# A macaron encoder step on one core: the down stages by seven products take their operands back by token halves

## The chip, the core and the metric

The kernel runs on one core of a Trainium2 chip. TensorE (PE) multiplies, VectorE (DVE), ScalarE (ACT) and GpSimd (POOL) work beside it, SyncE (SP) issues most transfers, GpSimd's queue the rest. The metric is the device time of one execution in microseconds (us); lower is better.

## The reference

One layer of a streaming encoder, for 16 meta tokens, 1024 prompt frames and 32 sample frames of 1024 channels:

```python
def half_ffn(x, g, w_gate, w_up, w_down):
    h = rmsnorm(x, g)
    return x + 0.5 * ((jax.nn.silu(h @ w_gate) * (h @ w_up)) @ w_down)

x = half_ffn(x, ffn1_norm, ffn1_w_gate, ffn1_w_up, ffn1_w_down)
h = rmsnorm(x, mix_norm)          # then h @ w_in: attention, HGRN2 branch, gates
x = x + merged @ w_out
x = half_ffn(x, ffn2_norm, ffn2_w_gate, ffn2_w_up, ffn2_w_down)
y = rmsnorm(x, final_norm)        # prompt and sample frames
```

The change touches the two products with `w_down` (2816 x 1024), and the norm that follows each.

## The kernel before

Every fp32 operand is split into a high and a low part, and a product is three matmuls (high x high, high x low, low x high). The two FFNs work by Strassen-like recursion: seven products for a 2 x 2 block product, with sums of operands named A11, S1 to S4 on the weight side and B11, T1 to T4 on the token side (`NAMES`). The tokens of an FFN form four quarters of 268 (first FFN) or 264 columns (second); `b` is the half (two quarters), `th` the quarter in it.

Each FFN is an object of class `Seven` (line 313). `rest` (L479) makes the gate and up products, block pair by block pair (11 of them, `i` = 0 to 10). `send` (L334) turns the result of a block into its seven operands: seven pieces of work in `self.later`, each a split into a staging tile `st` (tags R and st, one buffer each, in turn) and a store to `mid_dram` by GpSimd's queue (L349). They are done between later products, and those of block 10 in `down`.

`down` (L532) multiplies by `w_down`. `home(i)` (L488) loads the seven operands of block i into one of three places (`xh`/`xl` j with j = i mod 3, and one to three tiles more), names 0 to 2 in one transfer and 3 to 5 in another (0 and 1, 2 and 3 for j = 2). `lanes` (L501) loads a tile of `w_down` and makes the splits and sums for two blocks. A `Job` (L539) makes the seven products p1 to p7 for one pair of output blocks (`mp` 0 to 3), for one or two blocks of the inner dimension at a time; with `b` None for both halves, in pairs of PSUM banks (`pu`, `pv`, `pf`), else for one half in single banks (`ps_z`, `ps_o`). After p1 ScalarE copies `pv` to `pu` (L575); `out` (L559) adds results to `acc` by VectorE (L566), or writes them by ScalarE the first time (L569). `run` (L602) interleaves: p6 and p7 of a job stand among p1 to p5 of the next; at the end they are made alone.

Order before: block 0 alone for mp 2 and 3 (b None, pair banks), then steps s = 1 to 9 with blocks s-1 and s, mp 0 and 1 in odd and 2 and 3 in even steps, each step loading block s+1; a residual is added in most steps (L621). Then single banks: for each half four jobs (blocks 9 and 10 for mp 2 and 3, block 10 alone for mp 0 and 1), and after each half `after(b)`. In the first FFN that is `after1` (L810): store x1 and `normalise` (L230) the finished token tiles of 400, 384 and 288 columns; after both halves `between` starts the first scaling, and `project_all` (L829) follows with the first three column blocks of `w_in`. In the second it is `after2` (L1699): for each block of 128 tokens eight transposes, two squares with sums by ScalarE, a scale, two writes of `yt` by VectorE and a store of the output.

`PE` keeps the order of TensorE's matmuls as written (class `InOrder`, L91) where it is on; all other engines' orders are set by a planner from program order, dependencies and free buffers.

## Time and profile before

| | us |
|---|---|
| median of 3 runs | 2516.28 (2516.27 to 2518.82) |
| the profiled execution | 2516.3 |
| its span, first to last instruction | 2514.5 |
| TensorE busy in the span | 2411.5 (96%) |
| VectorE busy | 1680.1 (67%) |
| ScalarE busy | 1019.9 (41%) |
| GpSimd busy | 230.9 (9%) |
| mean granted TensorE clock, share of full speed | 0.985 |

The first down stage runs from 512.6 to 767.2 us of the span, the second from 2229.6 to 2491.4 us, with the output norm of the second half behind it. A busy TensorE is read with care, since matmuls are pipelined; the timelines show the idle time ahead of each instruction in brackets, with what ended it. "Before" a row in time says little on its cause: an engine works its queue in order.

### The profile page before, as it was taken

To read this page: it belongs to the slowest core of one execution; us is meant where nothing else is said; L and a number is where in the kernel's file an instruction comes from. 1 tells how busy PE (TensorE), PEld (TensorE's weight loads), DVE (VectorE), ACT (ScalarE), POOL (GpSimd) and SP (SyncE) were. 2 spreads that over 40 slices of the span, in tenths; PEclk is the share of its full clock that TensorE was granted. 3 is DMA by queue.
4 is the path that set the end of the run, shared out by engine and by line. 5 is a ranking of instruction groups with operands and counts; after the bars stand their busy time and mean duration, and the time that the engine had idled before them with its cause. 6 is when DMAs were issued, how large, how long until landed. Compare 5 with 4: busy or idle time off the path is not lost.

```text
span 2514.5 us, 47920 instructions
## 1 busy us (share of the span) xinstructions
PE 2411.5 (96%) x19500; PEld 2303.7 (92%) x19500; DVE 1680.1 (67%) x3160; ACT 1019.9 (41%) x2113; POOL 230.9 (9%) x461
## 2 busy tenths in 40 slices
PE   6999999989997999999999999999899999989996
PEld 5999999989997998898888888998899999989995
DVE  5876767668775377764666665557876776757775
ACT  6444444442234233332555544333444444443222
POOL 1000100000003012121000000111000000000000
PEclk9999999999998999999999999999999999999997
DMA  7234444487742111111111222522243434387741
GB/s 204 96 139 150 140 151 142 159 342 262 251 145 65 58 44 47 56 50 51 52 44 44 59 61 80 180 94 89 91 146 128 155 139 154 139 302 279 255 166 70
DMA packets 266020, 331.94 MB, mean 132 GB/s; under 512 B 41078, under 2 KB 228726, under 8 KB 260166
## 3 DMA queue, kind: packets, MB, share of 16 engines
q1 hardware_dynamic: 243590, 244.96, 29.9%
q0 software_dynamic: 22208, 83.91, 8.4%
q8 instruction: 153, 2.51, 0.4%
q14 instruction: 69, 0.57, 0.1%
HBM read 213.93 MB, written 114.89 MB: 131 GB/s over the span
## 4 chain that ended last, share of the span: by engine, by line
PE 54%; issue 31%; DVE 7%; POOL 3%; DMA 3%; ACT 2%; SPq 0%; POOLq 0%; DVEq 0%; ACTq 0%
PE ps_mm L103 20%; PE ps_z L103 12%; PE pu L103 6%; PE ps_o L103 5%; PE pf L103 4%; PE pv L103 4%; POOL mid_dram L349 3%; PE ps_tr L103 2%; PE ps_tr L106 2%; DMA mid_dram<-st 1%; DMA raw<-in_ffn_w_down_dram 1%; PE ps_z L106 1%; PE ps_mm L106 1%; DVE wlo L203 1%; DVE xl L235 0%
## 5 line engine op out<-in xcount | busy, mean ns | idle before, releaser
L103 PE MATMUL ps_mm<-xh,whi 128*128 128x384 f32 (+2 forms) x952 | 316.8, 333 | 0.5 <-DVE raw L1392 0.5
L103 PE MATMUL ps_mm<-xh,wlo 128*128 128x384 f32 (+2 forms) x952 | 310.3, 326 | 0.0
L103 PE MATMUL ps_mm<-xl,whi 128*128 128x384 f32 (+2 forms) x952 | 309.9, 326 | 0.0
L219 ACT ACTIVATE whi<-S 128x1024 fp32r<-128x1024 f32 x124 | 131.4, 1060 | 311.3 <-PE pu L103 157.8
L103 PEld LDWEIGHTS ps_mm<-xh,whi 128*128 128x128 f32 x952 | 179.3, 188 | 9.0 <-issue 5.0
L103 PEld LDWEIGHTS ps_mm<-xl,whi 128*128 128x128 f32 x952 | 179.3, 188 | 1.1
L103 PEld LDWEIGHTS ps_mm<-xh,wlo 128*128 128x128 f32 x952 | 179.5, 189 | 0.4
L220 DVE TENSOR_TENSOR wlo<-S,whi 128x1024 fp32r<-128x1024 f32 x124 | 151.7, 1223 | 37.5 <-ACT whi L219 34.8
L220 DVE TENSOR_TENSOR st<-g,st 128x536 fp32r<-128x536 f32 (+1 forms) x154 | 107.6, 709 | 101.2 <-ACT st L219 100.8
L349 POOL DMA_DIRECT2D mid_dram<-st x154 | 82.3, 534 | 904.4 <-DVE st L220 843.5
L1184 DVE TENSOR_TENSOR_SCAN left<-left,oneb 128x512 f32<-128x512 f32 (+6 forms) x112 | 107.4, 959 | 55.0 <-ACT left L119 54.6
L202 ACT ACTIVATE whi<-raw 128x1024 fp32r<-128x1024 f32 x67 | 70.5, 1057 | 175.9 <-PE ps_mm L103 136.3
L219 ACT ACTIVATE st<-g 128x536 fp32r<-128x536 f32 (+1 forms) x154 | 96.9, 642 | 88.4 <-DMA mid_dram<-st 75.1
L220 DVE TENSOR_TENSOR wlo<-raw,whi 128x1024 fp32r<-128x1024 f32 x80 | 76.6, 958 | 73.2 <-ACT whi L219 71.5
L103 PE MATMUL ps_z<-xl1s,whi 128*128 128x268 f32 (+1 forms) x424 | 116.8, 288 | 0.7 <-DVE acc1s L566 0.7
L103 PE MATMUL ps_z<-acc1s,whi 128*128 128x268 f32 (+1 forms) x480 | 106.3, 285 | 0.0
L103 PE MATMUL ps_z<-xh1s,whi 128*128 128x268 f32 (+1 forms) x360 | 102.8, 286 | 0.0
L103 PE MATMUL ps_z<-xh1s,wlo 128*128 128x268 f32 (+1 forms) x360 | 102.6, 285 | 0.0
L103 PE MATMUL ps_z<-xh2s,whi 128*128 128x268 f32 (+1 forms) x352 | 100.3, 285 | 0.9 <-ACT s L454 0.9
L103 PE MATMUL ps_z<-xl2s,whi 128*128 128x268 f32 (+1 forms) x352 | 100.3, 285 | 0.0
L103 PE MATMUL ps_z<-xh2s,wlo 128*128 128x268 f32 (+1 forms) x352 | 100.1, 285 | 0.0
L203 DVE TENSOR_TENSOR wlo<-raw,whi 128x1024 fp32r<-128x1024 f32 x67 | 83.2, 1246 | 25.3 <-ACT whi L202 25.1
(674 smaller groups left out, 7636.0 us busy)
## 6 DMA issues: line engine op xcount, KB each, us to landing
mid_dram<-st POOLq DMA_DIRECT2D x77, 536.0 KB, 3.8
mid_dram<-st POOLq DMA_DIRECT2D x77, 528.0 KB, 3.8
raw<-in_ffn_w_gate_dram SPq DMA_DIRECT2D x44, 512.0 KB, 3.8
raw<-in_ffn_w_up_dram SPq DMA_DIRECT2D x44, 512.0 KB, 3.9
raw<-in_w_in_dram SPq DMA_DIRECT2D x44, 512.0 KB, 3.7
raw<-in_ffn_w_down_dram SPq DMA_DIRECT2D x40, 512.0 KB, 3.8
u_xe<-mid_dram SPq DMA_DIRECT2D x14, 536.0 KB, 4.9
u_mh<-mid_dram SPq DMA_DIRECT2D x14, 528.0 KB, 5.1
```

Of the source, the lines that this page charges most:

```text
L103: return self.queue(nc.tensor.matmul(*args, **more))
L106: return self.queue(nc.tensor.transpose(*args, **more))
L202: A.activation(hi, raw, AF.Copy)
L203: V.tensor_tensor(lo, raw, hi.bitcast(F32), op=ALU.subtract)
L219: A.activation(dst_h, src, AF.Copy)
L220: V.tensor_tensor(dst_l, src, dst_h.bitcast(F32), op=ALU.subtract)
L349: nc.gpsimd.dma_start(self.mids[i, :, x], st.rearrange("p a b n -> p (a b) n").bitcast(F32))
L1184: V.tensor_tensor_scan(rev(st[:rows]), rev(st[:rows]), one, 1.0 if carry is None else carry[:rows], op0=ALU.mult, op1=ALU.mult)
```

## The change

Both uses of `down` change; the number of products and matmuls does not.

- `mid_dram` holds each block's operands by half, then by name. Class `Home` loads names 0 to 5 (0 to 3 for j = 2) of one half per transfer, and each further tile in one transfer of both halves.
- The first step, block 0 for mp 2 and 3, is made half by half in single banks; the pair banks come after it. Blocks 0 and 1 are loaded first half first. Four of block 10's stores are made ahead of the first step, three behind it, with staging in R, st and two `s` tiles. The weights of the next job (`ahead`) are made before the first step.
- Steps run to s = 10; steps 9 and 10 have one job each (mp 0, mp 2). The rest comes last, half by half in one `run` of six jobs: blocks 9 and 10 for mp 3, block 10 for mp 0, blocks 8 to 10 for mp 1. The last job's p3 and p4 change places, and its p6 stands ahead of p5.
- `after(0)` is called when the first half's last p7 is made. In the second FFN it returns four row blocks of the output norm, and `run` puts one behind every fifth product; the other five rotate through all single banks. `yt` uses tag gb.
- In the first FFN the first projection weights are made ahead of the last jobs, and the norm's two sums use the tags ms and ys with one buffer each.
- Two residuals are added in steps 4 and 5, none in steps 8 and 9.

```diff
         for first, last, eng in ((0, 5, G), (5, KC, V)):
-            tot = temp(pool, "tot")
+            tot = temp(pool, "ys" if tots else "ms", 1)
...
     x2_dram = dram.tile([P, KC, T], F32, name="x2_dram")
-    mid_dram = [dram.tile([FC // 2, P, 7, 4, qw], F32, name=f"mid{j}_dram") for j, qw in enumerate((QW, QW2))]
+    mid_dram = [dram.tile([FC // 2, P, 2, 7, 2, qw], F32, name=f"mid{j}_dram") for j, qw in enumerate((QW, QW2))]
...
             self.gs, self.later, self.groups = [], [], 0
+            self.stages = ["R", "st", "s", "s", "R", "st", "s"]
...
                         V.tensor_tensor(v, left, right, op=ALU.subtract)
-                    x = NAMES.index(name)
-                    if x % 2:
-                        st = base.tile([P, 2, 2, self.qw], F32R, tag="R", name="st")
+                    at = self.stages.pop(0) if i == FC // 2 - 1 else ("R", "st")[len(self.later) % 2]
+                    shape = [P, 2, 2, self.qw]
+                    if at == "R":
+                        st = base.tile(shape, F32R, tag="R", name="st")
+                    elif at == "st":
+                        st = self.pool.tile(shape, F32R, tag="st", name="st", bufs=1)
                     else:
-                        st = self.pool.tile([P, 2, 2, self.qw], F32R, tag="st", name="st", bufs=1)
-                    split(st[:, 0], st[:, 1], v)
-                    nc.gpsimd.dma_start(self.mids[i, :, x], st.rearrange("p a b n -> p (a b) n").bitcast(F32))
+                        st = self.tile(at, shape, F32R)
+                    split(st[:, :, 0], st[:, :, 1], v)
+                    nc.gpsimd.dma_start(self.mids[i, :, :, NAMES.index(name)], st.bitcast(F32))
...
+        class Home:
+            def __init__(self, ff, i):
+                self.ff, self.i, self.at = ff, i, {}
+            def load(self, b):
+                ff, j = self.ff, self.i % 3
+                tag, n = ((("xh0", 6), ("xh1", 6)), (("xl0", 6), ("xl1", 6)), (("xh2", 4), ("xl2", 4)))[j][b]
+                t = base.tile([P, n, 2, ff.qw], F32R, tag=tag, name=f"u_{tag}")
+                nc.sync.dma_start(t.bitcast(F32), ff.mids[self.i, :, b, 0:n])
+                for x in range(n):
+                    self.at[NAMES[x], b] = t[:, x]
+            def load_rest(self):
+                ff, j = self.ff, self.i % 3
+                x = 6 if j < 2 else 4
+                for tag, bufs in ff.homes[j]:
+                    t = ff.pool.tile([P, 2, 2, ff.qw], F32R, tag=tag, name=f"u_{tag}", bufs=bufs)
+                    nc.sync.dma_start(t.bitcast(F32), ff.mids[self.i, :, :, x])
+                    for b in range(2):
+                        self.at[NAMES[x], b] = t[:, b]
+                    x += 1
...
-            j = i % 3
-            tiles = [slots(tag, j, F32R, None, self.qw) for tag in ("xh", "xl")]
-            for tag, n in self.homes[j]:
-                tiles.append(self.pool.tile([P, 1, 4, self.qw], F32R, tag=tag, name=f"u_{tag}", bufs=n))
-            places = []
-            for t in tiles:
-                x, n = len(places), t.shape[1]
-                nc.sync.dma_start(t.bitcast(F32), self.mids[i, :, x:x + n])
-                places += [t[:, y] for y in range(n)]
-            return dict(zip(NAMES, places))
+            h = self.Home(self, i)
+            for b in range(2):
+                h.load(b)
+            h.load_rest()
+            return h
...
             a11, a12, a21, a22 = (r[:, :, k, h] for h in range(2) for k in range(2))
-            ah, al = own if own else [self.tile("g", [P, 3, 2, P], F32R) for _ in range(2)]
+            ah, al = [self.tile(own[0] if own else "g", [P, 3, 2, P], F32R) for _ in range(2)]
...
             V.tensor_tensor(s[:, 3], a12, s[:, 1], op=ALU.subtract)
-            sh = wp.tile([P, 4, 2, P], F32R, tag="whi", name="whi")
-            sl = wp.tile([P, 4, 2, P], F32R, tag="wlo", name="wlo")
+            if own and own[1]:
+                sh, sl = [self.tile(own[1], [P, 4, 2, P], F32R) for _ in range(2)]
+            else:
+                sh = wp.tile([P, 4, 2, P], F32R, tag="whi", name="whi")
+                sl = wp.tile([P, 4, 2, P], F32R, tag="wlo", name="wlo")
...
-        def down(self, w, resid, final, after, between):
+        def down(self, w, resid, final, after, early):
...
             class Job:
-                def __init__(job, W, units, mp, b=None):
-                    job.W, job.units, job.mp, job.b = W, units, mp, b
+                def __init__(job, units, mp, b=None):
+                    job.units, job.mp, job.b, job.done = units, mp, b, None
...
                         to = ps[:, b, :qw] if job.b is None else ps[:, :qw]
-                        for u, (unit, lane) in enumerate(job.units):
-                            (wh, wl), v = job.W[a], unit[x]
-                            for j, (p, q) in enumerate(((wh, b), (wh, 2 + b), (wl, b))):
+                        for u, (unit, W, lane) in enumerate(job.units):
+                            (wh, wl), v = W[a], unit.at[x, b]
+                            for j, (p, q) in enumerate(((wh, 0), (wh, 1), (wl, 0))):
...
                         to = acc[m][:, 2 * job.b + th]
-                    if (m, th) in begun:
+                    if (m, th, job.b) in begun or (m, th, None) in begun or (m, th, 0) in begun and job.b is None:
...
                     else:
-                        begun.add((m, th))
+                        begun.add((m, th, job.b))
...
+                queue, count = [], [0]
+                def step(product):
+                    product()
+                    count[0] += 1
+                    if queue and count[0] % 5 == 0:
+                        queue.pop(0)()
...
                 for job in jobs:
-                    job.p1()
+                    step(job.p1)
                     if before:
-                        before.p6()
-                    job.p2()
-                    job.p3()
+                        step(before.p6)
+                    step(job.p2)
+                    step(job.p4 if job.done == "end" else job.p3)
                     if before:
-                        before.p7()
-                    job.p4()
-                    job.p5()
+                        step(before.p7)
+                        if before.done:
+                            queue += before.done()
+                    step(job.p3 if job.done == "end" else job.p4)
+                    if job.done == "end":
+                        step(job.p6)
+                    step(job.p5)
                     before = job
-                before.p6()
+                if before.done != "end":
+                    before.p6()
                 before.p7()
+                while queue:
+                    queue.pop(0)()
...
+            def sends(n):
+                for _ in range(n):
+                    self.later.pop(0)()
+            PE.on = True
+            W = self.lanes(w, ((0, 2), (0, 3)))
+            units.update({i: self.Home(self, i) for i in range(2)})
+            for i in range(2):
+                units[i].load_rest()
+                units[i].load(0)
+            sends(4)
+            for i in range(2):
+                units[i].load(1)
+            ahead = self.lanes(w, ((0, 0), (1, 0)), ("raw2", None))
+            run([Job([(units[0], W, l)], 2 + l, b) for b in range(2) for l in range(2)])
+            sends(3)
+            adds = {2: (0,), 3: (4,), 4: (1, 2), 5: (5, 6), 6: (3,), 7: (7,)}
             def steps():
-                units[0] = self.home(0)
-                W = self.lanes(w, ((0, 2), (0, 3)))
-                while self.later:
-                    self.later.pop(0)()
-                units[1] = self.home(1)
-                for l in range(2):
-                    yield Job(W, [(units[0], l)], 2 + l)
-                for s in range(1, last):
+                for s in range(1, last + 1):
                     for mp in ((0, 1) if s % 2 else (2, 3)):
-                        if mp % 2 == 0:
+                        if s == last - 1 and mp == 1 or s == last and mp == 3:
+                            continue
+                        if mp % 2 == 0 and s < last:
                             units[s + 1] = self.home(s + 1)
-                        W = self.lanes(w, ((s - 1, mp), (s, mp)))
-                        if mp % 2 and s > 1:
-                            add_residual((s - 2) // 2 + (4 if s % 2 else 0))
-                        yield Job(W, [(units[s - 1], 0), (units[s], 1)], mp)
+                        W = ahead if s == 1 and mp == 0 else self.lanes(w, ((s - 1, mp), (s, mp)))
+                        if mp % 2:
+                            for m in adds.get(s, ()):
+                                add_residual(m)
+                        yield Job([(units[s - 1], W, 0), (units[s], W, 1)], mp)
...
             psum("pairs")
-            PE.on = True
...
             psum("singles")
-            Ws = [self.lanes(w, ((last - 1, mp), (last, mp))) for mp in (2, 3)]
-            Ws.append(self.lanes(w, ((last, 0), (last, 1)),
-                                 [self.tile("raw2", [P, 3, 2, P], F32R) for _ in range(2)]))
+            W3 = self.lanes(w, ((last - 1, 3), (last, 3)))
+            W1 = self.lanes(w, ((last - 2, 1), (last - 1, 1)))
+            W01 = self.lanes(w, ((last, 0), (last, 1)), ("raw2", "s"))
             functions(final)
+            if early:
+                early()
+            jobs = []
             for b in range(2):
-                jobs = [Job(Ws[x], [(units[last - 1], 0), (units[last], 1)], 2 + x, b) for x in range(2)]
-                jobs += [Job(Ws[2], [(units[last], l)], l, b) for l in range(2)]
-                run(jobs)
-                after(b)
-            between()
+                u8, u9, u10 = (units[last - 2 + x] for x in range(3))
+                jobs += [Job([(u9, W3, 0), (u10, W3, 1)], 3, b), Job([(u10, W01, 0)], 0, b),
+                         Job([(u8, W1, 0), (u9, W1, 1), (u10, W01, 1)], 1, b)]
+            jobs[2].done, jobs[5].done = lambda: after(0), "end"
+            run(jobs)
+            for work in after(1):
+                work()
...
         fed = {}
-        homes.update(tot=("s", 2), sq=("S", 2))
+        homes.update(sq=("S", 2))
+        def early1():
+            fed["w"] = weights([(w_in[0][:, COL_ZF:COL_ZF + P], KC)])
...
         def after1(b):
-            if not fed:
+            if "R" not in fed:
...
-        ff.down(ffn1_w_down, x0_dram, "natural_log_exp_and_others", after1, lambda: waiting.pop(0)())
+            return []
+        ff.down(ffn1_w_down, x0_dram, "natural_log_exp_and_others", after1, early1)
+        waiting.pop(0)()
...
-        def project_all(units, tiles=TT, rotate=False, between=None):
-            ws = [weights([(w_in[0][:, col:col + P], KC)]) for col, _ in units]
+        def project_all(units, tiles=TT, rotate=False, between=None, ahead=()):
+            ws = list(ahead) + [weights([(w_in[0][:, col:col + P], KC)]) for col, _ in units[len(ahead):]]
...
         PE.on = True
-        project_all([zf_unit(h) for h in range(3)], TT, True, lambda: waiting and waiting.pop(0)())
+        project_all([zf_unit(h) for h in range(3)], TT, True, lambda: waiting and waiting.pop(0)(),
+                    [fed["w"]])
...
-        ready, found = [0], []
+        found = []
...
             if not found:
-                gfin = base.tile([P, D], F32, tag="R", name="gfin")
-                nc.sync.dma_start(gfin, final_norm[None, :].to_broadcast([P, D]))
-                found.append(gfin)
-            gfin = found[0]
+                found.append(base.tile([P, D], F32, tag="R", name="gfin"))
+                nc.sync.dma_start(found[0], final_norm[None, :].to_broadcast([P, D]))
+            gfin, = found
             acc = [a.rearrange("p q n -> p (q n)") for a in ff.acc]
-            while ready[0] < 9:
-                j = ready[0]
-                c0, r = (N_META + j * P, P) if j < 8 else (SAMP0, NS)
-                if c0 + r > N_META + (half + 1) * 2 * QW2:
-                    break
-                ready[0] += 1
-                yt = pool.tile([P, D], F32, tag="mh", name="yt", bufs=4)
+            def rows(j):
+                c0, r = (j * P, P) if j < 8 else (SEQ, NS)
+                yt = pool.tile([P, D], F32, tag="gb", name="yt")
...
                 for hf in range(2):
-                    ps = bank(("mm", "mm", "tr")[rot[0] % 3])
-                    rot[0] += 1
+                    ps = bank(rotate=True) if half else bank(("mm", "mm", "tr")[rot[0] % 3])
+                    rot[0] += not half
                     for k in range(4):
-                        PE.transpose(ps[:r, k * P:(k + 1) * P], acc[4 * hf + k][:, c0 - N_META:c0 - N_META + r], ident)
+                        PE.transpose(ps[:r, k * P:(k + 1) * P], acc[4 * hf + k][:, c0:c0 + r], ident)
...
-        ff.down(ffn2_w_down, x2_dram, "sqrt_and_others", after2, lambda: None)
+            return [lambda j=j: rows(j) for j in (range(4, 9) if half else range(4))]
+        ff.down(ffn2_w_down, x2_dram, "sqrt_and_others", after2, None)
...
```

## Rows read from the trace of the kernel before

**Rows 1.** the page of the profile, its first line

```profile
span 2514.5 us, 47920 instructions
```

**Rows 2.** the chain of work that ended last: start us, us, what; steady steps

```profile
546.47 1.48 PE pv L103 x12
...
2421.09 1.46 PE pv L103 x12
```

**Rows 3.** windows by stage: stretch, its length, busy us (instructions), TensorE's clock, DMA

```profile
512.58:532.66 20.08, 12.68 (x74) 11.68 (x72) 9.87 (x16) 8.07 (x15) 2.13 (x4) 0.83 0.94 379
725.24:767.24 42.00, 36.31 (x254) 34.42 (x255) 28.93 (x65) 19.14 (x39) 4.18 (x4) 0.92 0.27 98
767.24:794.20 26.96, 18.04 (x85) 16.34 (x84) 15.04 (x20) 14.01 (x30) 16.17 (x16) 0.87 0.26 77
2229.60:2250.19 20.59, 12.74 (x73) 12.04 (x74) 9.61 (x15) 8.18 (x15) 2.13 (x4) 0.79 0.90 372
2442.54:2514.50 71.96, 48.56 (x324) 44.02 (x324) 36.72 (x85) 17.32 (x54) 0.00 (x0) 0.79 0.16 61
2459.55:2472.42 12.87, 6.17 (x34) 5.14 (x33) 5.64 (x13) 5.36 (x17) 0.00 (x0) 0.64 0.20 81
2491.42:2514.50 23.08, 7.75 (x42) 5.37 (x40) 9.06 (x21) 7.89 (x25) 0.00 (x0) 0.63 0.25 98
```

**Rows 4.** timeline of TensorE, first stage: start us, us, line, operation [idle before]

```profile
514.03 1.00 PE L103 MATMUL pv<-xh0s,g 128*128 128x268 f32 x6 [1.29 <-DVE g L432]
...
518.70 1.71 PE L103 MATMUL pv<-xh0s,g 128*128 128x268 f32 x6 [2.93 <-ACT pu L575]
...
742.04 0.52 PE L103 MATMUL ps_z<-u_xe,whi 128*128 128x268 f32 x2 [0.53 <-DVE acc1s L566]
...
758.57 0.81 PE L103 MATMUL ps_z<-u_xe,whi 128*128 128x268 f32 x2 [3.02 <-DVE acc2s L566]
...
777.66 0.70 PE L103 MATMUL ps_z<-xh,wlo 128*128 128x400 f32 x1 [8.92 <-DVE wlo L203]
```

**Rows 5.** timeline of ScalarE at the first stage's start

```profile
516.96 1.19 ACT L219 ACTIVATE st<-g 128x536 fp32r<-128x536 f32 x2 [4.66 <-DMA mid_dram<-st]
518.05 0.60 ACT L575 ACTIVATE pu<-pv 128x536 f32<-128x536 f32 x1
```

**Rows 6.** DMA issues of 500 to 517 us: count, size, us to landing

```profile
xh1s<-mid_dram SPq DMA_DIRECT2D x1, 1608.0 KB, 10.3
...
mid_dram<-st POOLq DMA_DIRECT2D x1, 536.0 KB, 10.0
```

**Rows 7.** timelines of ScalarE and VectorE behind the first stage

```profile
768.45 0.51 ACT L240 ACTIVATE t_s<-acc0s 128x384 f32<-128x384 f32 x1
...
775.07 0.55 DVE L244 TENSOR_TENSOR t_s<-t_s,t_S 128x384 f32<-128x384 f32 x1
...
776.40 2.35 DVE L203 TENSOR_TENSOR wlo<-raw,whi 128x1024 fp32r<-128x1024 f32 x2
```

**Rows 8.** end of the second stage: timelines of TensorE and VectorE, one row of the chain

```profile
2463.60 0.69 PE L106 MATMUL ps_tr<-cst,acc1s 128*128 128x128 f32 x2 [2.58 <-DVE yt L1729]
...
2462.79 0.75 DVE L1729 SCALAR_TENSOR_TENSOR yt<-ps_tr,rs,gfin 128x512 f32<-128x512 f32 x1
...
2495.39 0.74 DVE L1729 SCALAR_TENSOR_TENSOR yt<-ps_tr,rs,gfin 128x512 f32<-128x512 f32 x1
...
2464.23 2.60 DMA out_dram<-yt
```

**Rows 9.** timelines of SyncE's DMA queue and of TensorE, first stage

```profile
506.32 0.32 SPq L497 DMA_DIRECT2D xh1s<-mid_dram  x1
...
701.68 0.32 SPq L497 DMA_DIRECT2D xl1s<-mid_dram  x1
...
709.24 0.54 PE L103 MATMUL pv<-xh2s,g 128*128 128x268 f32 x3
```

**Rows 10.** DMA issues of 690 to 726 us: count, size, us to landing

```profile
xh1s<-mid_dram SPq DMA_DIRECT2D x1, 1608.0 KB, 6.6
```

## Prediction

> **What bounds the kernel now.** I read the profile's page first: span 2514.5 us [rows 1], TensorE far ahead of every other engine; so the question for every edit is whether TensorE waits there. Next, the timeline of TensorE through both down stages, which are the only code that the diff touches (with the norm behind each). In the middle of a stage the reader sees no gap: 12 matmuls take 1.48 us in the first stage and 1.46 us in the second, 0.1233 and 0.1217 us each [rows 2]. The losses sit at the two ends, which the windows by stage isolate [rows 3]. The profiled run took 2516.3 us for its span of 2514.5 us, and the median of the timed runs is 2516.28 us, so a microsecond of span is one of time.
>
> *Start of a stage.* From the last matmul of the gate/up work to the first product of the first block pair, 72 matmuls are issued in 20.08 us (first stage) and 20.59 us (second) [rows 3]. They need 72 x 0.1233 = 8.9 and 72 x 0.1217 = 8.8 us, so 11.2 and 11.8 us are lost. The timeline names the gaps [rows 4]: 1.29 us until the pair pool has its PSUM banks, 2.93 us until ScalarE has copied `pv` to `pu`; the rest is a further wait and a granted clock of 0.83 and 0.79 [rows 3]. Why was ScalarE late? Its row ahead of that copy is a split into staging `st`, which waited 4.66 us for an earlier store [rows 5]: 7 stores pass through two staging tiles, and a store landed after 10.0 us beside the loads [rows 6].
>
> *End of the first stage.* From the change to single banks to the last matmul, 42.00 us for 252 down matmuls (31.1 us) and 2 of the projection; VectorE is busy for 28.93 us of it [rows 3]. One wait of 3.02 us on an accumulation dominates [rows 4], then the clock falls. Behind it the projection waits 8.92 us for `wlo` [rows 4]: VectorE made it at 776.40, after the norm's work [rows 7].
>
> *End of the second stage.* 71.96 us [rows 3], of which 12.87 us lie between the halves (the norm of four row blocks, TensorE busy for 6.17 us) and 23.08 us behind the last product (five blocks). There each block waits for the bank of the one before it: 2.58 us until `yt` is written [rows 8].
>
> **The change part by part.** The product count is unchanged: 11 blocks x 4 output pairs x 7 products x 3 matmuls x 2 halves.
>
> *First steps by halves* (per stage). The pool hand-over moves behind the four half jobs. Four of the last block's seven stores now use R, st and two `s` tiles, so none waits on an earlier store; three come behind the half jobs. Before, these 84 matmuls took 20.08 us plus 12 x 0.1233 = 1.5 us for those left over: 21.6 us. After: 84 x 0.1233 = 10.4 us, plus a drained tail and the hand-over (0.53 and 1.29 us [rows 4], 1.7 taken), plus ScalarE: 20 half-width evictions between 0.30 us (half of the 0.60 us row) and 0.60 us, 0.4 taken, four splits of 0.6 us and the lanes worked out ahead (1792 columns, 2.0 us at 0.60 us for 536) make 12.4 us [rows 5], so 1.5 us over TensorE (0 to 2.3). The three later stores reuse R, st and `s`; their splits stand in ScalarE's queue, and behind them the copies that TensorE waits for, as at 516.96 and 518.05 [rows 5]. The bound is nothing to the 4.66 us seen now; 2.5 taken, with 1 us of low clock. That leaves 6.7 us of loss, so 21.6 - 10.4 - 6.7 = 4.5 us gained. Bounds: 9 (no wait) to -2 (the slot `xh1` for the second half of block 0 was loaded at 506.32 [rows 9], landing 10.3 us later [rows 6], at 516.6 us, and is wanted two half jobs in, at 512.6 + 5.2 = 517.8; two stores more ahead of it would use that up).
> The Trainium skill (DMA: Bandwidth & Descriptors, section Queues, rings and completion order) says that a DMA engine takes turns between its queue rows packet by packet. By that rule a store would share the engines with the loads at once; with the fit of the same page of the Trainium skill (section Anatomy of one DMA), 2.0 us plus bytes at 436 GB/s, halved here, a 536 KB store would land in an estimated 4.5 us. The measured 10.0 us [rows 6] is against it here, and the row decides the sum; by the rule the stores would be in time, and the start would gain 9 us per stage.
>
> *Loads by halves* (every step). The first load of a block could start when the third product was done with its slot; now both halves hold names up to T1, and are free only behind the sixth product, as `xl` was: 701.68 [rows 9]. The cover: the next step starts 2 jobs (168 x 0.1233 = 20.7 us) after the present one, the issue stands 2.7 us into it, 18.0 us remain, and two halves and a weight tile (3.8 MB) need 10 us at 379 GB/s [rows 3]. So nothing, with 6 to 8 us to spare. If the cover went, it would cost 18 steps. One place lacks it: block 10 was needed two jobs after its slot became free, and the new order has one job there (the odd pair comes last). Issue at 701.68, first half after 6.6 us [rows 10], second 4.2 us later at 379 GB/s: 712.5. TensorE wants it in the first product of the next job, at 709.24 [rows 9] plus 1.1 us: a stall of 2 us per stage (0 to 5).
> SyncE's queue keeps its order otherwise: the weight tiles stand behind the block's last tile as before. Two residuals instead of one in two steps cost nothing while VectorE keeps pace.
>
> *Last steps.* Six half jobs in one pipeline instead of two runs of four: no drained tail in the middle, 18 instead of 24 VectorE evictions per half, and the norm's destination `xh0`/`xl0` holds only first-half operands, so it is free when half 0 is done. First stage: 31.1 us plus 2.4 us (0.5 to 6: the norm's work still shares VectorE) = 33.5, against 42.0 less 0.7 for the two projection matmuls: 7.8 us gained (4 to 9.7).
>
> *Behind the first stage.* The first projection weights come early, which removes the 8.92 us wait [rows 4]. What is late next is the chain of the norm: squares start when the first sums have been taken, 768.45 to 775.62, 7.2 us [rows 7], while 24 projection matmuls take 18.04 x 24/85 = 5.1 us [rows 3]. So some 2.2 us of wait stay, 1 us for the second and third `wlo` (2.35 us for two [rows 7]) and 1 us of clock and restart; 26.96 us become 21.4: 5.5 us gained (9 to -2, below).
>
> *Norm between the products* (second stage). Four blocks go between the products: 32 transposes, at 0.12 us (the pitch of a matmul, rows 2) to 0.18 us (6.17 us over 34 [rows 3]), 4 us, plus 3 us while VectorE and ScalarE serve both, 252 x 0.1217 = 30.7 us of products: 37.7 us up to the last product. Behind it five blocks, with eight banks instead of three. The pace is then the output buffer: two tiles, each written in 1.4 us (two `yt` of 0.75, overlapped) and stored in 2.60 us [rows 8], 2.1 us a block; first block done after 4.9 us (2491.42 [rows 3] to 2496.13, and 0.2 for the last eviction [rows 8]), four more 8.4 us, landing and end 2.6 us: 15.9 us. In all 53.6 us against 71.96: 18.4 us gained (13 to 21).
>
> Sum: first stage 4.5 + 7.8 + 5.5 - 2 = 15.8; second 4.5 + 18.4 - 2 = 20.9; together 36.7. 2516.3 - 36.7 = 2479.6, say 2480 us.
>
> **Rivals.**
> *The staging wait stays, and the norm's chain takes over.* The late splits block ScalarE as now, and the shared `ms`/`ys` buffer goes to the scaling of the first tile before the next tile's sums, so the projection waits as before. For: one buffer where there were two, and the 10.0 us store. Against: the sums come first in the program. Without 2 x 4.5 and 5.5 us: 2494 us.
> *The norm between the products starves the evictions.* VectorE has 28.93 of 42.00 us in use at the first stage's end; with norm rows in front of evictions the second stage's end would keep only the 23.08 - 15.9 = 7.2 us behind its last product: 2516.3 - 15.8 - (4.5 + 7.2 - 2) = 2491 us.
> *Stores in time.* The start gains 9 us per stage: 2471 us. The rule of the Trainium skill quoted above (DMA: Bandwidth & Descriptors) gives this result.
> *Slower: loads late in every step.* Two halves and a weight tile must land in 18.0 us; at 379 GB/s they take 10, at 180 GB/s 21, which is 2.6 us late (settling ignored) in 18 steps: 47 us, 2526 us. It outweighs the gain below some 185 GB/s. Against it: the loads at the start ran at 379 and 372 GB/s [rows 3].
> *It does nothing:* the gaps only move, 2512 to 2520 us. Against: the 12.87 us and the 8.92 us are removed by order alone.
>
> **How the numbers follow.** Forecast 0.55; staging and chain 0.13; starved evictions 0.12; stores in time 0.12; slower 0.04; nothing 0.04. The range takes in the first four and the bounds above, which partly offset each other: 2463 to 2499 us. A measurement of this kernel tells about 0.2% (5 us) from no change. Faster 0.92, same 0.04, slower 0.04.
>
> **What would show it.** Right: no half-clock stretch between the last gate/up matmul and the first pair; a wait of some 2 us on the halves of block 10 in the last pair step; four blocks of transposes among the last products; blocks about 2.1 us apart at the very end; the projection's first matmuls at once. Wrong: waits on loads in the middle steps, ScalarE's splits waiting on stores among the half jobs, the projection's sums waiting for a free buffer.

## The result, and the profile after

| | us |
|---|---|
| before, median of 4 runs | 2517.55 (2516.27 to 2522.13) |
| after, median of 4 runs | 2501.01 (2499.49 to 2503.65) |
| ratio | 0.9932, 95% interval 0.9915 to 0.9949 |
| the profiled execution of after | 2499.49, span 2497.4 |

The change makes the kernel faster, by 16.5 us. Predicted were 36.7 us and a range that ended at 2499: the sign is right, the size is less than half.

I lay the two traces side by side by stretches that hold the same matmuls. The stretches of before start and end at the rows of [rows 3]; those of after at its first half job, its change to single banks, and the mixer's fourth projection.

| stretch | before | after | after - before | predicted |
|---|---|---|---|---|
| up to the last gate/up matmul | 512.58 | 518.38 | +5.8 | 0 |
| stage 1, first step and middle | 212.66 | 218.77 | +6.1 | -2.5 |
| stage 1, last steps and behind | 68.96 | 58.49 | -10.5 | -13.3 |
| mixer and gate/up of stage 2 | 1435.40 | 1436.11 | +0.7 | 0 |
| stage 2, first step and middle | 212.94 | 213.70 | +0.8 | -2.5 |
| stage 2, last steps and norm | 71.96 | 51.95 | -20.0 | -18.4 |

In these two executions the ends gained about what was forecast. The starts, forecast as a gain, lost. Each figure is that of one execution. The starts repeat where runs below have the same code there (e3, e6, e10: 26.8 to 27.2 us in stage 1, 26.2 to 28.3 in stage 2); the end of stage 1 does not (e1, e3, e10: 60.8 to 64.6 us), and that of after, 58.49, is the shortest.

The windows of after by stage, as in [rows 3] (stretch, its length, busy us and instructions of TensorE, its weight loads, VectorE, ScalarE and GpSimd, TensorE's granted clock, DMA share, GB/s): first half jobs, last half jobs, what stands behind them; then the first half jobs and the end of stage 2.

```profile
518.38:545.68 27.30, 16.46 (x86) 14.18 (x84) 14.10 (x26) 12.32 (x30) 4.17 (x6) 0.81 0.94 362
737.15:776.89 39.74, 34.76 (x256) 33.47 (x257) 27.47 (x54) 17.84 (x36) 6.98 (x6) 0.96 0.42 141
776.89:795.64 18.75, 15.92 (x82) 14.48 (x81) 10.60 (x17) 11.35 (x24) 9.19 (x9) 1.00 0.17 56
2231.75:2257.61 25.86, 16.07 (x86) 14.27 (x84) 14.13 (x26) 12.28 (x30) 4.17 (x6) 0.80 0.88 347
2445.45:2497.40 51.95, 39.87 (x324) 38.53 (x324) 30.33 (x73) 16.35 (x51) 0.00 (x0) 0.93 0.21 84
```

The same 84 matmuls took about 21.6 us before; now they take 27.30 us. The timeline of TensorE in that stretch names two long waits, both on ScalarE; below them the two of stage 2:

```profile
524.12 1.04 PE L103 MATMUL ps_z<-u_xh,g 128*128 128x268 f32 x3 [4.84 <-ACT ps_z L600]
...
536.62 0.65 PE L103 MATMUL ps_o<-u_xh,g 128*128 128x268 f32 x3 [3.31 <-ACT acc1s L594]
...
2237.97 1.03 PE L103 MATMUL ps_z<-u_xh,g 128*128 128x264 f32 x3 [5.33 <-ACT ps_z L600]
...
2250.30 0.63 PE L103 MATMUL ps_o<-u_xh,g 128*128 128x264 f32 x3 [1.27 <-ACT acc1s L594]
```

And ScalarE's timeline of stage 1 says what it did instead:

```profile
517.03 1.06 ACT L219 ACTIVATE whi<-S 128x1024 fp32r<-128x1024 f32 x1 [1.77 <-PE ps_z L103]
523.14 0.65 ACT L219 ACTIVATE st<-g 128x536 fp32r<-128x536 f32 x1 [5.04 <-DMA mid_dram<-st]
523.69 0.38 ACT L600 ACTIVATE ps_z<-ps_z 128x268 f32<-128x268 f32 x1
...
535.64 0.65 ACT L219 ACTIVATE st<-g 128x536 fp32r<-128x536 f32 x1 [3.69 <-DMA mid_dram<-st]
536.19 0.38 ACT L594 ACTIVATE acc1s<-ps_o 128x268 f32<-128x268 f32 x1
```

The split at 523.14 is B22's: the only staged operand besides B11 and B21 that needs no subtraction first. In the program it stands behind the half jobs (`sends(3)`); in ScalarE's queue the planner set it ahead of their first copy (`ps_z`, L600). It reuses R, whose store (of B11) was issued at 512.78 and landed 10.3 us later. The split at 535.64 is that of T2, in `st`, and waits for the store of T1. Stores land late here:

```profile
mid_dram<-st POOLq DMA_DIRECT2D x4, 536.0 KB, 8.2
...
mid_dram<-s POOLq DMA_DIRECT2D x2, 536.0 KB, 9.5
```

Those are the DMA issues of 510 to 540 us, median us to landing in the last column. So the wait of [rows 5] has not gone. Before had two such waits of TensorE in each first step: 2.93 us [rows 4] and one of 2.86 us that came by way of VectorE, whose row stood behind a split; in stage 2, 3.64 and 2.90 us (before; VectorE, then TensorE):

```profile
528.20 0.72 DVE L220 TENSOR_TENSOR st<-g,st 128x536 fp32r<-128x536 f32 x1 [4.28 <-ACT st L219]
...
529.60 0.52 PE L103 MATMUL pu<-u_xe,whi 128*128 128x268 f32 x2 [2.86 <-DVE acc1s L566]
...
2236.28 1.69 PE L103 MATMUL pv<-xh0s,g 128*128 128x264 f32 x6 [3.64 <-ACT pu L575]
...
2246.85 0.51 PE L103 MATMUL pu<-u_mh,whi 128*128 128x264 f32 x2 [2.90 <-DVE acc1s L566]
```

After has two again, longer in stage 1 and as long in sum in stage 2. They stand in front of half jobs, which have a single bank where a pair job had two, and shorter waits for evictions come on top.

### The profile page after: what moved, and what is told of

The parts are those of the page before. It is cut to its first block, busy times and chain, and to the rows that moved or that the text cites. A ratio compares the mean times of both kernels' runs of the same rounds, so it can differ in the third digit from the quotient of the medians.

```text
span 2497.4 us, 47900 instructions
## 1 busy us (share of the span) xinstructions
PE 2403.0 (96%) x19500; PEld 2299.1 (92%) x19500; DVE 1669.2 (67%) x3144; ACT 1021.3 (41%) x2129; POOL 257.2 (10%) x461
## 4 chain that ended last, share of the span: by engine, by line
PE 54%; issue 29%; DVE 6%; DMA 4%; POOL 4%; ACT 3%; POOLq 0%; SPq 0%; DVEq 0%; ACTq 0%
PE ps_mm L103 20%; PE ps_z L103 11%; PE pu L103 6%; PE ps_o L103 5%; PE pv L103 4%; PE pf L103 4%; POOL mid_dram L353 3%; DMA mid_dram<-st 2%; PE ps_tr L103 2%; PE ps_tr L106 2%; PE ps_z L106 1%; DMA u_xl<-mid_dram 1%; DVE wlo L203 1%; PE ps_mm L106 0%; DVE acc L1661 0%
## 5 line engine op out<-in xcount | busy, mean ns | idle before, releaser
L353 POOL DMA_DIRECT2D mid_dram<-st x148 | 102.7, 702 | 872.7 <-DVE st L220 854.9
L103 PE MATMUL ps_z<-xl1s,whi 128*128 128x268 f32 (+1 forms) x360 | 102.6, 285 | 0.0
## 6 DMA issues: line engine op xcount, KB each, us to landing
u_xh<-mid_dram SPq DMA_DIRECT2D x8, 1608.0 KB, 10.4
```

The lines of the kernel that those rows point to most:

```text
L103: return self.queue(nc.tensor.matmul(*args, **more))
L353: nc.gpsimd.dma_start(self.mids[i, :, :, NAMES.index(name)], st.bitcast(F32))
```

## The experiments

Theory A: the place of the late splits in ScalarE's queue costs the start. Rivals: the half jobs cost by themselves (B), or operands land late (C). Medians; ratios against the kernel before, measured beside each.

| run | us | ratio | 95% interval |
|---|---|---|---|
| e1_pin | 2481.33 | 0.9862 | 0.9849 to 0.9876 |
| e2_oldfirst | 2497.34 | 0.9931 | 0.9916 to 0.9945 |
| e3_lump | 2512.10 | 0.9984 | 0.9975 to 0.9993 |
| e4_layout | 2516.07 | 1.0000 | 0.9992 to 1.0009 |
| e6_noearly | 2504.76 | 0.9952 | 0.9939 to 0.9964 |
| e7_beforepin | 2516.32 | 1.0003 | 0.9994 to 1.0012 |
| e8_later | 2485.82 | 0.9883 | 0.9870 to 0.9897 |
| e9_sums | 2480.26 | 0.9851 | 0.9838 to 0.9865 |
| e10_banks | 2508.33 | 0.9956 | 0.9943 to 0.9970 |
| e11_oldpin | 2490.57 | 0.9891 | 0.9877 to 0.9904 |

**e1_pin: the late splits held behind the half jobs.**

```diff
-        A.activation(dst_h, src, AF.Copy)
+        i = A.activation(dst_h, src, AF.Copy).ins
+        if hold[0] is not None:
+            tc.add_manual_dep(i, hold[0].name, order, reason="order")
...
+            hold[0] = evict[0]
             sends(3)
+            hold[0] = None
```

(`evict[0]` is the last ScalarE eviction that a job has issued.)

> The changed kernel, with the splits of the last three staged operands (B22, T2, T4 of the last block) held in ScalarE's queue behind the last ScalarE eviction of the half jobs, in both stages; nothing else differs. Theory A (in the changed kernel the split of B22 stands ahead of the half jobs' first evictions and waits 5.04 us for a staging buffer whose store is on its way, and a second one 3.69 us; TensorE stands 4.84 and 3.31 us behind them): both waits go, the 84 half-job matmuls take 17 to 19 us instead of 27.3 in stage 1, and some 4 less than 24 in stage 2, so about 2487 us (2484 to 2491). Rival B (the half jobs cost by themselves: single banks, twice as many evictions): the idle time moves to the waits for ps_z and acc evictions, 2497 to 2502. Rival C (the operands land too late, the DMA engines are full at about 410 GB/s there): TensorE waits for u_xh and u_xl instead, the start is 22 to 25 us, 2493 to 2497.

2481.33 us, 19.7 less than the change (17.6 by the ratios) and below the 2484 to 2491 that A had asked for. The windows of both first steps, then ScalarE where B22's split had stood:

```profile
514.47:531.65 17.18, 13.85 (x86) 12.26 (x84) 10.65 (x21) 11.01 (x28) 2.09 (x3) 0.90 1.01 405
2220.66:2237.12 16.46, 13.63 (x87) 12.11 (x85) 10.61 (x21) 10.77 (x28) 2.06 (x3) 0.90 1.01 422
```

```profile
513.13 1.06 ACT L221 ACTIVATE whi<-S 128x1024 fp32r<-128x1024 f32 x1 [1.76 <-PE ps_z L103]
515.04 0.38 ACT L604 ACTIVATE ps_z<-ps_z 128x268 f32<-128x268 f32 x1 [0.85 <-PE ps_z L103]
```

The eviction no longer stands behind a waiting split. The steps take 17.18 and 16.46 us instead of 27.30 and 25.86, the clock stands at 0.90 instead of 0.81 and 0.80, and no wait on an operand appears, so B and C fall. Of 17.18 us TensorE is idle for 3.3 (17.18 less the 13.85 busy), in short waits for evictions: the half jobs cost something by themselves, but far less than B had. The stores are no faster in it: between 506 and 535 us they land after 10.3 and 10.9 us, beside 405 GB/s. Only who stands behind them has changed.

**e2_oldfirst and e11_oldpin: the old first step, without and with held splits.**

```diff
-            units.update({i: self.Home(self, i) for i in range(2)})
...
-            run([Job([(units[0], W, l)], 2 + l, b) for b in range(2) for l in range(2)])
-            sends(3)
+            W0 = self.lanes(w, ((0, 2), (0, 3)))
+            units[0] = self.home(0)
+            sends(7)
+            units[1] = self.home(1)
...
+                for l in range(2):
+                    yield Job([(units[0], W0, l)], 2 + l)
```

(In e11_oldpin `sends(4)` stands there, and `hold` around `sends(3)` behind the two jobs.)

> The changed kernel with the first step of each down stage put back: two jobs over both halves of the tokens, block 0's operands all loaded first, then the seven stores, then block 1's operands; last steps, store layout, staging buffers and norm as changed. If the new first step as built is what lost the time (theory A and rival B alike): the stretch from the last gate/up matmul to the third job is again near 20 us in both stages instead of 27.3 and 24.3, about 2490 us (2488 to 2493). If the store layout or the order of the last steps lost it (rival D): the start stays some 25 us or the loss stands elsewhere, 2497 to 2502.

> The changed kernel with the first step put back to two jobs over both halves and whole loads of a block (e2_oldfirst), four stores ahead of block 1's loads, and the last three splits held in ScalarE's queue behind the first two jobs' evictions issued by then (e1_pin's edit); last steps and the rest as changed. If the half jobs and half loads themselves gain what the prediction had given them (4.5 us a stage less 2): 2485 to 2491 us. Rival (only the place of the splits and the four staging buffers mattered, the halves nothing): within 3 us of e1_pin, 2479 to 2484 us.

e2 took 2497.34 us, some 4 us above what A and B gave it, and inside the range of rival D (2497 to 2502). The old first step was not back at its old length: from the last gate/up matmul its 72 matmuls took about 25 us in both stages, before 20.08 and 20.59. That is the length D had named, but not for D's reasons: e4 below finds no cost of the layout alone, and the timeline shows the copies waiting behind splits as in [rows 4], and a wait on a load besides:

```profile
517.80 1.04 PE L103 MATMUL pv<-u_xh,g 128*128 128x268 f32 x3 [2.25 <-DMA u_xh<-mid_dram]
522.81 1.71 PE L103 MATMUL pv<-u_xh,g 128*128 128x268 f32 x6 [2.64 <-ACT pu L600]
533.83 1.32 PE L103 MATMUL pv<-u_xh,g 128*128 128x268 f32 x6 [4.21 <-ACT pu L600]
```

e11 separates the two. With the splits held, 2490.57 us, in the range of the first theory and 9.2 above e1 (7.3 by the ratios). The largest wait left at the start is for the load of the second half of block 0, wanted right behind the first; one row from each stage:

```profile
517.47 0.65 PE L103 MATMUL pv<-u_xh,g 128*128 128x268 f32 x3 [2.16 <-DMA u_xh<-mid_dram]
...
2232.28 1.03 PE L103 MATMUL pv<-u_xh,g 128*128 128x264 f32 x3 [4.08 <-DMA u_xh<-mid_dram]
```

So halves and half loads, with the next job's weights made ahead, are worth some 4 us a stage (2.5 and 5.2 by the traces, first step and middle together), but only where ScalarE isn't held up: without the hold the change, at 2501.01 us, is no faster than e2.

**e7_beforepin: the same hold in the kernel before.** Two sends ahead of block 1's loads, two jobs, five sends held.

> The kernel before, with the splits of the last five staged operands held in ScalarE's queue behind the last ScalarE eviction of the first two jobs that is issued ahead of them, in both stages. Theory A for the kernel before (a split that waits for a staging buffer stands ahead of the first jobs' evictions there too; TensorE waits 2.93 and 3.64 us for pu behind it): those waits go, 3 to 6 us a stage less the half clock that they left behind, 2504 to 2511 us. Rival (over both halves of the tokens the first jobs are bound by the landing of block 0's and block 1's operands: the next job then waits for its loads instead): 2514 to 2518 us.

No gain, 2516.32 us. With two staging buffers for five splits the wait only went on to the next job, whose weight splits now stand behind a staging split: the first steps are 4.9 and 7.1 us shorter than before, the middle steps 5.3 and 5.1 longer. ScalarE, then TensorE:

```profile
528.19 0.65 ACT L221 ACTIVATE st<-g 128x536 fp32r<-128x536 f32 x1 [2.58 <-DMA mid_dram<-st]
```

```profile
529.20 0.51 PE L103 MATMUL pv<-xh0s,g 128*128 128x268 f32 x2 [4.10 <-ACT g L221]
```

The rival's number held, its reason (loads) did not: no wait on a load stands there. The hold paid in e1 and e11, which both have the change's extra staging buffers and where no held split waits for a store; e2 and the change itself have the buffers without the hold, and both wait in their first steps.

**e3_lump and e10_banks: the end of stage 2.**

```diff
-                            queue += before.done()
+                            for work in before.done():
+                                work()
```

```diff
-                    ps = bank(rotate=True) if half else bank(("mm", "mm", "tr")[rot[0] % 3])
-                    rot[0] += not half
+                    ps = bank(("mm", "mm", "tr")[rot[0] % 3])
+                    rot[0] += 1
```

> The changed kernel, with the first half's row norms of stage 2 issued in one lump right behind the first half's last product instead of one after every five products; nothing else differs. If the end of stage 2 gains by the norm lying between products: four rows of eight transposes stand in a row on TensorE and each pair waits for its bank and the square sums, some 2 to 2.5 us a row, so 8 to 10 us longer, 2508 to 2511 us. Rival (the gain of about 20 us at that end comes from the order of the steps and from the free banks in the second half, and the lump is covered): 0 to 3 us longer, 2500 to 2504.

> The changed kernel, with the row norms of the last five rows in stage 2 again on the three banks of mm and tr instead of the rotation over eight; nothing else differs. If the free banks matter at that end: each row's transposes wait for the scaled output of the row before, up to 2.06 to 2.6 us a row as in the lump of e3_lump, for three of the five rows, 4 to 7 us longer, 2505 to 2508 us. Rival (square sums, roots and output transfers end last there, whatever the banks): 0 to 2 us, 2500 to 2503 us.

The lump costs 11.1 us (13 by the ratios), a little more than expected, the three banks 7.3 us (6), at the top of what was expected. Both show the wait of [rows 8], which after has at neither place beyond 0.44 us; first e3_lump between the halves, then e10_banks behind the last product:

```profile
2470.41 0.44 PE L106 MATMUL ps_tr<-cst,acc1s 128*128 128x128 f32 x2 [2.59 <-DVE yt L1789]
2473.86 0.69 PE L106 MATMUL ps_mm<-cst,acc1s 128*128 128x128 f32 x2 [2.13 <-DVE yt L1789]
2477.89 0.69 PE L106 MATMUL ps_mm<-cst,acc1s 128*128 128x128 f32 x2 [2.06 <-DVE yt L1789]
```

```profile
2490.77 0.44 PE L106 MATMUL ps_mm<-cst,acc1s 128*128 128x128 f32 x2 [2.12 <-DVE yt L1788]
2494.21 0.69 PE L106 MATMUL ps_mm<-cst,acc1s 128*128 128x128 f32 x2 [2.12 <-DVE yt L1788]
...
2502.25 0.61 PE L106 MATMUL ps_mm<-cst,acc1s 128*32 128x128 f32 x2 [2.05 <-DVE yt L1788]
```

**e4_layout: the store layout alone, in the kernel before.**

> The kernel before, with the changed layout of the staged operands in memory alone (halves of tokens outermost, so a store goes in two pieces of 2144 bytes a partition instead of one of 4288, and a load in two pieces a partition); all orders as before. In the changed kernel the gate/up matmuls of stage 1 end 5.8 us later than before. Theory (the layout makes the stores slower, and the splits that wait for them hold ScalarE): 4 to 7 us longer in stage 1, the same or less in stage 2, 2520 to 2528 us. Rival (the 5.8 us are of that one execution): within 2 us of the kernel before.

Nothing: 1.0000, so the layout by itself costs the kernel no 5.8 us. Nine executions whose program up to there is that of the change had the last gate/up matmul at 513.1 to 518.5 us, with 518.26 in after; with the old program it stood at 512.46 in before and 513.92 in e7, with the new layout alone at 515.24 in e4. Most of the 5.8 us is scatter of one execution, and what remains I can't name.

**e6_noearly: no early projection weights.**

> The changed kernel without the early load and split of the first mixer weights in stage 1 (they are again made behind the down stage); nothing else differs. If the prediction's term for what stands behind stage 1 is right: TensorE waits again for wlo ahead of the mixer's first matmuls, up to the 8.9 us of before, so 4 to 9 us longer than the changed kernel, 2505 to 2510 us. Rival (the norm sums of the second half end last there, whose waits of 1.63 and 1.20 us the changed kernel shows, so the weights are ready in time anyway): 0 to 2 us, 2500 to 2503.

2504.76 us, 3.8 more (5.0 by the ratios), between the two, with intervals that overlap. In the trace `wlo` is waited for nowhere at that place, so the theory's mechanism falls. The last steps and what stands behind them take 60.04 us against 58.49, less than in e1, e3 and e10, which have the early weights. The profiled executions differ most in stretches that have the same code (mixer and start of stage 2 longer, the part ahead of stage 1 shorter), so a cost of leaving the early weights out is not shown.

**e8_later and e9_sums: the wait of 3.9 us inside the last steps.** Both stand on e1_pin's held splits. TensorE, after:

```profile
762.37 1.39 PE L103 MATMUL ps_tr<-t_ms,cst 128*128 128x400 f32 x2 [3.90 <-POOL t_ms L244]
...
783.06 0.91 PE L103 MATMUL ps_o<-t_ms,cst 128*128 128x384 f32 x2 [1.63 <-POOL t_ms L244]
785.17 0.91 PE L103 MATMUL ps_o<-t_ys,cst 128*128 128x384 f32 x2 [1.20 <-DVE t_ys L244]
```

```diff
-            return []
+            return [] if b else [lambda: None, lambda: None, waiting.pop(0)]
...
-        waiting.pop(0)()
```

```diff
-        for first, last, eng in ((0, 5, G), (5, KC, V)):
+        for first, last, eng in ((0, 5, G if t0 else V), (5, KC, V)):
```

> The kernel with the held splits (e1_pin), and in stage 1 the two ones-matmuls of the first token tile put in TensorE's written order fifteen products behind the first half's last product, where the planner had set them some five behind it and TensorE stood 3.90 us for the sum on GpSimd with the clock at half behind that; nothing else differs. If that wait is worth its length: 4 to 6 us less than e1_pin, 2475 to 2478 us. Rival (the shared buffers of the norm sums: the second token tile's sums can only start when the first tile's scale is done, now later, and TensorE waits there for what it saved here): 2480 to 2483 us.

> The kernel with the held splits (e1_pin), and in stage 1 the first token tile's five-chunk square sum added on VectorE instead of GpSimd; nothing else differs. In e1_pin and e8_later two VectorE operations that lie beside GpSimd's additions take 2.71 us where two such took 1.17, and an addition 1.05 instead of 0.56, and TensorE stands 3.9 or 3.35 us behind these engines. If the two engines hinder each other: VectorE's operations are short again, the ones-matmul waits 0 to 2 us instead of 3.9, and the kernel takes 2 to 4 us less than e1_pin, 2477 to 2479 us. Rival (VectorE is the engine that ends last there, and four more additions of 0.56 us make it later): 0 to 3 us more than e1_pin, 2481 to 2484 us.

Later ones-matmuls (the sums over partitions) gained nothing: 2485.82 us is above e1 and above both ranges. The wait kept its place and changed its name, but not to the shared sum buffer of the rival:

```profile
748.70 0.65 PE L103 MATMUL ps_z<-u_xh,whi 128*128 128x268 f32 x2 [3.35 <-DVE acc2s L595]
```

VectorE was as late as GpSimd, since its rows beside GpSimd's additions are long. VectorE in e8_later, then in e9_sums, where GpSimd is idle:

```profile
743.95 1.17 DVE L239 SCALAR_TENSOR_TENSOR xl<-acc1s,gains,xh 128x400 fp32r<-128x400 f32 x2
...
745.59 2.71 DVE L239 SCALAR_TENSOR_TENSOR xl<-acc2s,gains,xh 128x400 fp32r<-128x400 f32 x2
748.23 0.42 DVE L595 SCALAR_TENSOR_TENSOR acc2s<-ps_z,acc2s 128x268 f32<-128x268 f32 x1
748.57 1.05 DVE L248 TENSOR_TENSOR t_ys<-t_ys,t_S 128x400 f32<-128x400 f32 x1
```

```profile
748.32 1.17 DVE L239 SCALAR_TENSOR_TENSOR xl<-acc2s,gains,xh 128x400 fp32r<-128x400 f32 x2
749.42 0.56 DVE L248 TENSOR_TENSOR t_ms<-t_ms,t_S 128x400 f32<-128x400 f32 x1
```

So the two engines do hinder each other, but the time doesn't show it: in e9 the wait is 2.30 us and the end of stage 1 takes 57.94 us instead of e1's 61.52, a stretch in which runs of one code differ by more (58.49 in after, 64.57 in e10). The time is 2480.26 us, between the two ranges and within the interval of e1. It is the lowest of all, though not told apart from e1.

## Why the prediction was wrong, step by step

**What bounds the kernel:** right. What the traces name as won or lost at the two ends of a stage are TensorE's waits and its lower clock behind them.

**First steps by halves: the step that failed.** The text said that "three come behind the half jobs", and for their splits "the bound is nothing to the 4.66 us seen now; 2.5 taken, with 1 us of low clock". It named the mechanism, but took the program's order for the queue's and bounded it by one wait. Only TensorE's order is written by hand here, ScalarE's is the planner's, and the planner set B22's split ahead of the first copy. Two waits came in each stage, as before the change: 4.84 + 3.31 us in the first, 5.33 + 1.27 in the second, with a low clock behind them (0.52 between 537.3 and 541.6 us). The step took 27.30 and 25.86 us, not 17.1. From 21.6 and 22.1 us (20.59 plus the 1.5 left over) the starts lost 5.7 and 3.8 us instead of gaining 4.5: 18.5 of the missing 19.6 us.

With the splits behind the half jobs in the queue too, e1 took 17.18 and 16.46 us, and the whole kernel 2481 against the 2480 forecast. Part of that agreement is luck. e1 has no staging wait, so the sum without its 2.5 gives 14.6; the other 2.6 and 1.9 us went to waits for evictions and to a clock of 0.90, for which too little had been taken. And in e1 the end of stage 1 gained 7.4 us instead of 13.3, while the middle steps cost nothing where 4 were forecast. What e1 bears out of the rest is the 0.4 us taken for an eviction (0.38 in its row) and that nothing waits for `xh1`.

**The stores.** The rule of the Trainium skill (DMA: Bandwidth & Descriptors, section Queues, rings and completion order) led to an estimate of 4.5 us and to stores in time. While the engines were full the rows show more: medians of 8.2 and 9.5 us in after, 10.3 and 10.9 us in e1. One store of after, issued at 537.33 where the DMA share had fallen to 0.65, landed after 4.2 us. Whether the queues take turns as the rule says, no run here shows.

**Loads by halves:** right. Apart from the place that was named, no middle step waits on a load. The predicted stall of 2 us where block 10 follows by one job came in both stages, within 0 to 5:

```profile
722.52 0.64 PE L103 MATMUL pv<-u_xl,g 128*128 128x268 f32 x3 [1.92 <-DMA u_xl<-mid_dram]
...
2430.72 0.64 PE L103 MATMUL pv<-u_xl,g 128*128 128x264 f32 x3 [0.66 <-DMA u_xl<-mid_dram]
```

**Last steps of stage 1:** the mechanism is right, the term mis-sized. For the norm's share 2.4 us were taken with 6 as the bound; 39.74 us less 31.1 make 8.6 (four matmuls of the norm included), of which 3.90 are the wait for GpSimd's sum, and VectorE's rows beside GpSimd are part of its length.

**Behind stage 1:** 18.75 us against 21.4 predicted, but not for the reason given. The early weights aren't what removed the 8.92 us: without them (e6) nothing waits for `wlo` either. The third pair of `whi`/`wlo` buffers, which the last jobs now leave free, may be; it wasn't tried. The sums' chain was late next as said, with 1.63 and 1.20 us. With the longer ends of e1, e3 and e10, the two parts together gained 4.4 to 8.1 us, not 13.3, so the 10.5 of after is in part a lucky execution.

**Norm between the products:** right, 20.0 us against 18.4. From the first of these products to the last passed 35.3 us (37.7 forecast), behind them 16.7 (15.9), with the last blocks 2.1 to 2.5 us apart. e3 and e10 price its two parts at 11.1 and 7.3 us; they aren't parts of a sum, since each was taken away alone.

**Slips in the sums on record.** 12.4 less 10.4 is 2.0, not 1.5, and 18.04 with 2.2, 1 and 1 on top is 22.2, not 21.4. Put right, they take 1.8 us off the 36.7, which explains little of the miss.

**The rivals.** The first half of "the staging wait stays" is what happened, worse than it was priced (2 x 4.5); its second half, the shared buffer, did not. A chance of 0.13 was too little for a case whose sign in the trace, splits among the half jobs, the prediction itself had named. The missing 19.6 us are 18.5 of the starts, 5.8 ahead of stage 1, 2.8 at its end and 0.7 in the mixer, less 6.6 in the middle steps and 1.6 at the end of stage 2. The 5.8, 2.8 and 0.7 are of the size by which executions of one code differ; why the middle steps came out shorter than forecast, by 5 us in stage 2, stays open.

## What to carry to other kernels

A step moved in the program moves in a queue only where the queue's order is written down; ask of every engine whose order is planned what may be set ahead of the work that the bound engine waits for, and pin instructions that wait on a slow transfer. An ordering edge (an instruction set behind another in the queue, with no wait of its own) was worth 17.6 to 19.7 us, more than the change. A wait that ends beside another engine's equal lateness, as in e8, gained nothing when it was moved: look at what is late next first.

## What was not expected of the hardware

VectorE and GpSimd hinder each other. Two VectorE operations of 400 columns with both inputs in SBUF take 1.17 us alone and 2.71 beside GpSimd's additions, an addition 1.05 instead of 0.56 (rows of e8 and e9 above). Three of GpSimd's additions take 3.79 us there, where one takes 1.04 (GpSimd, e1):

```profile
737.95 1.04 POOL L248 TENSOR_TENSOR t_ms<-t_ms,t_S 128x400 f32<-128x400 f32 x1 [200.84 <-ACT t_ms L244]
745.01 3.79 POOL L248 TENSOR_TENSOR t_ms<-t_ms,t_S 128x400 f32<-128x400 f32 x3 [6.03 <-ACT t_S L247]
```

The Trainium skill (SBUF — State Buffer, section Who interferes with whom) says that a VectorE instruction with two SBUF inputs contends with a GpSimd instruction that reads SBUF, because its second input comes through a read interface that the two share. These lengths agree with that, but no run shows the interface itself.
